# x's row sums on ScalarE, no two-input work on GpSimd, 512-token plain units, and an output projection by columns

## The chip, the core and the metric

The kernel runs on one core of a Trainium2 chip. Its engines are TensorE (PE, matmuls; PEld is its weight load), VectorE (DVE), ScalarE (ACT), GpSimd (POOL) and SyncE (SP), which here only issues DMAs. The metric is device microseconds of one execution; the median of three runs is given. Times in the text are microseconds (us) from the first instruction of the profiled execution.

## The reference

x is 512 tokens x 2048. One decoder layer is computed in float32:

- h = x * rsqrt(mean(x^2) + 1e-6) * gain, then z = h @ w_in with w_in 2048 x 8192.
- z is split into eight blocks of 1024 columns. Four (q, f, i, g) feed 8 heads of HGRN2, a gated linear recurrence with a 128 x 128 state; four (q, k, v, g) feed 16 heads of causal attention with ALiBi, in which three dilated windows are mixed.
- Each branch is multiplied by silu of its gate g; both are laid side by side to y (512 x 2048), then x + y @ w_out, and a last RMSNorm.

## The kernel before

**Arithmetic.** Each float32 operand of a large product is cut into a high and a low part (`cut`, L107 on ACT and L108 on DVE) and a product is three matmuls: hi*hi, hi*lo, lo*hi (L653 to L655, L725 to L727, L955 to L957, L985 to L987).

**Input projection.** The 8192 columns are worked in 32 units of 256 columns (two blocks of 128). x comes transposed in 16 tiles `xt` of 128 features x 512 tokens and is cut by `split_x`. Units 0 to 3 are "plain": 16 steps k, and in each step two blocks x two token halves of 256 (tiles X1, A21, X2, X4), 12 matmuls of 256 columns, in four PSUM banks. The other 28 units use seven products over half-size blocks in place of eight (Strassen's scheme), 24 matmuls of 256 columns each; they need the sums X3, X5, X6, X7, which are built on DVE during units 1 to 3. x's norm is applied after the projection: the row sums of squares are formed beside unit 0 (`square_x`: ACT squares each `xt`, POOL adds into `acc`, a matmul with ones at L248 sums over features), and `rrow` scales each result.

**Mixers.** While the projection of later units runs, the heads of the finished units run in its gaps. Their parts are put at slots by `at_slot(dt, fn)`; `tick()` counts one slot per 12 matmuls of a product (per step k in a plain unit). A HGRN head's `carry` has three two-input multiplies on POOL (L371 to L373), an attention pair's `bias` one scaling and one addition on POOL (L483, L484). `turn` and `turn_values` are PE transposes that wait for a result of DVE or ACT. Each result y goes to DRAM (`y_dram`).

**Output projection.** Columns 0 to 1023 are plain: four passes (kh, n), each over one half of the features and 512 columns, with four PSUM banks that are added into `r` (x, loaded from DRAM) at L960 after each pass. Columns 1024 to 2047 use seven products again. y is read back from DRAM and cut: `y_hgrn` (for kh = 0), `y_attn` (kh = 1), `y_sums` (the sums for the products). `open_out1` loads x's second half, `open_out2` the final gain `fg`, and multiplies the eight finished `r` tiles by it on POOL (L892). `finish` scales the rows and stores.

**Order.** Each engine and each DMA queue runs its instructions in a fixed order. That order is made before the run: a planner takes the program's order and its own estimate of durations, so that an instruction may be issued ahead of earlier ones that are not ready in its estimate; at run time a late input holds up all that is queued behind.

Of the kernel before, what the change touches and what calls it, by code (L numbers as in the profile page):

```python
# [63 lines left out]
def tile_kernel(ctx: ExitStack, tc: tile.TileContext, x, xT, w_in, w_out, gain, lbl, gnorm, fgain,  # L64
# [45 lines left out]
    def x_tiles(m, of=None):  # L110

        return [tuple(xp.tile([P, 4, HS], F32R, tag=f"X{of or m}{p}{t}", name=f"X{m}{p}{t}") for p in "hl")
                for t in range(2)]

# [11 lines left out]
    acc = st.tile([P, S], F32, name="acc")  # L126
    xts = []

    def load_x(upto):
        while len(xts) < min(upto, KT):  # L130
            k = len(xts)
            xt = st.tile([P, S], F32, tag="xt", name=f"xt_{k}", bufs=13)
            nc.sync.dma_start(xt, xT[k * P:(k + 1) * P, :])
            xts.append(xt)

    X = {m: x_tiles(m) for m in (1, 2, 4, 7)}
    A21 = x_tiles(3)
    for m in (6, 5):
        X[m] = x_tiles(m)

    def blocks_of(k):

        return (X[1], A21) if k < KH else (X[2], X[4])

    def split_x(k):
        t, kb = divmod(k % KH, 4)
        g = gain_sb[:, k:k + 1]
        for th, pair in enumerate(blocks_of(k)):
            hi, lo = (a[:, kb] for a in pair[t])
# [4 lines left out]
    def square_x(k):  # L154
        if k == 0:
            A.activation(acc, xts[k], AF.Square)
        else:
            sq = st.tile([P, S], F32, tag="sq", name=f"xsq_{k}", bufs=2)
            A.activation(sq, xts[k], AF.Square)
            G.tensor_add(acc, acc, sq)  # L160

    def x7(k):
        t, kb = divmod(k, 4)
        hi, lo = (a[:, kb] for a in X[7][t])
        g, d = gain_sb[:, k:k + 1], st.tile([P, HS], F32, tag="d7", name=f"d7_{k}", bufs=3)
        V.tensor_sub(d, xts[k][:, :HS], xts[k][:, HS:])
        A.activation(hi, d, AF.Copy, scale=g)
        V.scalar_tensor_tensor(lo, d, g, hi.bitcast(F32), op0=ALU.mult, op1=ALU.subtract)
# [21 lines left out]
    def x3(t):  # L190
        if t == 0:
            X[3] = x_tiles(3)
# [51 lines left out]
    def row_stats():  # L244

        ss = mixer_bank("ss_ps")
        for sb in range(NSB):
            T.matmul(ss[:, sb:sb + 1], acc[:, sb * P:(sb + 1) * P], cs["ones"][:, 0:1], start=True, stop=True)  # L248
        ms = cst.tile([P, NSB], F32, name="ms_x")
        V.tensor_scalar(ms, ss[:, :NSB], 1.0 / D, EPS, op0=ALU.mult, op1=ALU.add)  # L250
# [106 lines left out]
    def work_v(h, src):  # L357
# [5 lines left out]
        def carry():  # L363
# [93 lines left out]
    def work_aq(j, q):  # L457
# [21 lines left out]
        def bias(i):  # L479
# [3 lines left out]
            G.tensor_scalar(nb, H["dist"][:, 0], slope, 0.0, op0=ALU.mult, op1=ALU.add)  # L483
            G.tensor_add(nb, nb, H["dist"][:, 1])  # L484
# [49 lines left out]
    def work_av(j, src):  # L534
# [18 lines left out]
        at_slot(1, turn_values)  # L553
        at_slot(12, values)
# [63 lines left out]
    def plain_unit(u):  # L618
        blocks = UNITS[u]
        banks = [[bank(*tb) for tb in (("a", f"a_{u}"), ("c", f"c_{u}"))],  # L620
                 [bank(*tb) for tb in (("c", f"c2_{u}"), ("t", f"t_{u}"))]]
        for k in range(KT):
            kg, kb = divmod(k, 4)
            t = kg % 2
            if u == 0:
                load_x(k + 8)
                if k == 1:
                    load_plain(0, 1)
                    small_consts()
                for i in range(*((0, 2) if k == 0 else (k + 1, min(k + 2, KT)))):  # L630
                    split_x(i)
                if k >= 1:
                    for i in range(*((0, 1) if k == 1 else (k - 1, k))):
                        square_x(i)
# [12 lines left out]
            for n in range(2):  # L647
                hi, lo = pieces[u, kg, n]
                c = slice(kb * P, kb * P + P)
                for th, pair in enumerate(blocks_of(k)):  # L650
                    xh, xl = (a[:, kb] for a in pair[t])
                    ps = banks[n][th][:, :HS]
                    T.matmul(ps, hi[:, c], xh, start=k == 0, stop=False)  # L653
                    T.matmul(ps, hi[:, c], xl, start=False, stop=False)
                    T.matmul(ps, lo[:, c], xh, start=False, stop=k == KT - 1)  # L655
        if u == 0:
            square_x(KT - 1)
# [3 lines left out]
        for n, (kind, i, _) in enumerate(blocks):  # L661
            z = block_tile(kind, i)
            A.copy(z[:, :HS], banks[n][0][:, :HS])
            V.tensor_copy(z[:, HS:], banks[n][1][:, :HS])
# [93 lines left out]
    Y = {}  # L758
    O = {}

    def staged(k, pool, tag):
        s = pool.tile([P, S], F32, tag=tag, name=f"ys_{k}_{now[0]}", bufs=2)
        nc.sync.dma_start(s, y_dram[k])
        return s
# [5 lines left out]
    def y_tiles(*which):  # L770
        for m, of in which:
            if m not in Y:
                Y[m] = x_tiles(m, of)

    def y_hgrn(kb):
        y_tiles((21, 7), (1, 1))
        h = staged(kb, zp, "zA" if kb % 2 else "zB")
# [3 lines left out]
    def y_attn(kb):  # L781
        y_tiles((2, 2), (4, 4))
        a = staged(KH + kb, O["w2"], "ya")
        cut(*y_parts(2, kb), a[:, :HS])
        cut(*y_parts(4, kb), a[:, HS:])

    def y_sums(kb):

        y_tiles((7, 3), (5, 5), (6, 6), (3, 7))
        h, a = staged(kb, O["w2"], "yh"), staged(KH + kb, O["w2"], "ya")  # L790
        a11, a21, a12, a22 = h[:, :HS], h[:, HS:], a[:, :HS], a[:, HS:]
        V.tensor_sub(a11, a11, a21)
        cut(*y_parts(7, kb), a11)
        V.tensor_sub(a21, a22, a21)
        V.scalar_tensor_tensor(a22, a11, -1.0, a22, op0=ALU.mult, op1=ALU.subtract)
        cut(*y_parts(6, kb), a22)
        V.scalar_tensor_tensor(a12, a12, -1.0, a22, op0=ALU.mult, op1=ALU.subtract)
        cut(*y_parts(3, kb), a12)
        cut(*y_parts(5, kb), a21)

    def after_product(u, m):
        if u == len(UNITS) - 1 and m in (6, 3, 5, 4):
            i = (6, 3, 5, 4).index(m)
            y_hgrn(2 * i)
            y_hgrn(2 * i + 1)
# [7 lines left out]
    OS = [(0, (kh, n), jb) for kh in range(2) for n in range(2) for jb in range(4)]  # L813
# [22 lines left out]
    osteps = [(0, (kh, n), kb) for kh in range(2) for n in range(2) for kb in range(KH)]  # L836
# [21 lines left out]
    def open_out():  # L858
        close(H["acm"])
        close(zp_cm)  # L860
# [4 lines left out]
        for th in range(2):  # L865
            for n in range(2):
                for blk in range(2):
                    r = w2.tile([P, 512], F32, name=f"r0_{th}_{n}_{blk}")
                    sb = 2 * th + blk
                    nc.sync.dma_start(r, x[sb * P:(sb + 1) * P, n * 512:n * 512 + 512])  # L870
                    O["R"][0, th, n, blk] = r

    def open_out1():

        for i, (th, n) in enumerate(((1, 1), (0, 0), (1, 0), (0, 1))):
# [230 lines left out]
```

## Time and profile before

| | |
|---|---|
| median of 3 runs | 1009.81 us (1009.49 to 1012.33) |
| profiled execution | 1009.9 us, span 1008.1 us |
| PE busy | 945.9 us, 94% of the span |
| PEld busy | 888.3 us, 88% |
| DVE busy | 779.3 us, 77% |
| ACT busy | 576.1 us, 57% |
| POOL busy | 199.0 us, 20% |
| mean granted TensorE clock | 0.981 |

A busy share is the part of the span in which an engine had an instruction under way. Matmuls are pipelined, so the distance between the starts of two matmuls, and not the duration of one, says what a matmul costs. In a row, "[2.59 <-DMA r<-x_dram]" is idle time before the instruction and what ended it.

### The profile page before, as it was taken

To read this page: it belongs to the slowest core of one execution; us is meant where nothing else is said; L and a number is where in the kernel's file an instruction comes from. 1 tells how busy PE (TensorE), PEld (TensorE's weight loads), DVE (VectorE), ACT (ScalarE), POOL (GpSimd) and SP (SyncE) were. 2 spreads that over 40 slices of the span, in tenths; PEclk is the share of its full clock that TensorE was granted. 3 is DMA by queue.
4 is the path that set the end of the run, shared out by engine and by line. 5 is a ranking of instruction groups with operands and counts; after the bars stand their busy time and mean duration, and the time that the engine had idled before them with its cause. 6 is when DMAs were issued, how large, how long until landed. Compare 5 with 4: busy or idle time off the path is not lost.

```text
span 1008.1 us, 18861 instructions
## 1 busy us (share of the span) xinstructions
PE 945.9 (94%) x7096; PEld 888.3 (88%) x7096; DVE 779.3 (77%) x1564; ACT 576.1 (57%) x1218; POOL 199.0 (20%) x203
## 2 busy tenths in 40 slices
PE   5899999999999999989999999999999998989795
PEld 5899999999999999988999999999999866768584
DVE  7899869787786878767878787888888835677756
ACT  7554456556464656556667676767666724345345
POOL 5501312121111211112121222221211101001501
PEclk9899999999999999999999999999999999989898
DMA  8133356676766666665666666666666649835634
GB/s 319 53 115 100 80 138 166 158 185 158 180 158 178 158 147 158 157 167 148 161 156 165 156 148 157 152 160 158 161 167 178 200 159 290 275 110 134 180 83 167
DMA packets 51516, 162.34 MB, mean 161 GB/s; under 512 B 5792, under 2 KB 5824, under 8 KB 51424
## 3 DMA queue, kind: packets, MB, share of 16 engines
q1 hardware_dynamic: 36576, 108.02, 31.5%
q0 software_dynamic: 14560, 52.58, 29.0%
q8 instruction: 56, 0.92, 0.4%
q10 hardware_dynamic: 288, 0.52, 0.2%
q14 instruction: 36, 0.29, 0.1%
HBM read 152.72 MB, written 8.39 MB: 160 GB/s over the span
## 4 chain that ended last, share of the span: by engine, by line
PE 62%; DVE 14%; DMA 10%; issue 8%; ACT 3%; POOL 2%; SPq 0%; DVEq 0%; POOLq 0%; ACTq 0%
PE a L725 6%; PE a L727 6%; PE a L726 6%; PE t L725 4%; PE t L727 4%; PE t L726 4%; DMA ys<-yd 3%; PE c L726 3%; PE c L725 3%; PE c L727 3%; DVE lo L108 3%; DMA wB<-w_in_dram 3%; PE ao L547 2%; PE op L955 2%; DVE lo_o L108 2%
## 5 line engine op out<-in xcount | busy, mean ns | idle before, releaser
L107 ACT CAST hi<-wA 128x512 fp32r<-128x512 f32 x168 | 103.3, 619 | 93.9 <-PE a L726 52.6
L108 DVE TENSOR_TENSOR lo<-wA,hi 128x512 fp32r<-128x512 f32 x168 | 114.7, 690 | 18.4 <-ACT hi L107 17.6
L108 DVE TENSOR_TENSOR lo<-wB,hi 128x512 fp32r<-128x512 f32 x112 | 85.5, 771 | 16.6 <-ACT hi L107 16.2
L107 ACT CAST hi<-wB 128x512 fp32r<-128x512 f32 x112 | 68.0, 615 | 49.3 <-PE a L726 19.7
L584 POOL DMA_DIRECT2D wA<-w_in_dram x56 | 49.5, 883 | 141.3 <-DVE lo L108 124.8
L682 DVE TENSOR_TENSOR wA<-wA,wB 128x512 f32<-128x512 f32 x56 | 39.4, 713 | 44.8 <-DMA wB<-w_in_dram 44.8
L725 PE MATMUL t<-X3h,hi 128*128 128x256 f32 x224 | 65.7, 293 | 0.0
L725 PE MATMUL c<-X4h,hi 128*128 128x256 f32 x224 | 65.3, 291 | 0.0
L725 PE MATMUL a<-X1h,hi 128*128 128x256 f32 x224 | 65.1, 291 | 0.0
L725 PE MATMUL a<-X5h,hi 128*128 128x256 f32 x224 | 64.9, 290 | 0.0
L725 PE MATMUL a<-X6h,hi 128*128 128x256 f32 x224 | 64.8, 289 | 0.1
L725 PE MATMUL t<-X2h,hi 128*128 128x256 f32 x224 | 64.1, 286 | 0.0
L725 PE MATMUL c<-X7h,hi 128*128 128x256 f32 x224 | 63.9, 285 | 0.0
L727 PE MATMUL t<-X3h,lo 128*128 128x256 f32 x224 | 63.9, 285 | 0.0
L726 PE MATMUL t<-X3l,hi 128*128 128x256 f32 x224 | 63.9, 285 | 0.0
L726 PE MATMUL a<-X1l,hi 128*128 128x256 f32 x224 | 63.5, 283 | 0.0
L727 PE MATMUL a<-X1h,lo 128*128 128x256 f32 x224 | 63.5, 283 | 0.0
L727 PE MATMUL a<-X6h,lo 128*128 128x256 f32 x224 | 63.4, 283 | 0.0
L727 PE MATMUL t<-X2h,lo 128*128 128x256 f32 x224 | 63.4, 283 | 0.0
L726 PE MATMUL t<-X2l,hi 128*128 128x256 f32 x224 | 63.4, 283 | 0.0
L726 PE MATMUL a<-X5l,hi 128*128 128x256 f32 x224 | 63.3, 283 | 0.0
L727 PE MATMUL c<-X7h,lo 128*128 128x256 f32 x224 | 63.3, 283 | 0.0
(389 smaller groups left out, 3523.0 us busy)
## 6 DMA issues: line engine op xcount, KB each, us to landing
wA<-w_in_dram POOLq DMA_DIRECT2D x56, 512.0 KB, 7.1
wB<-w_in_dram SPq DMA_DIRECT2D x28, 512.0 KB, 4.3
wA<-w_in_dram SPq DMA_DIRECT2D x28, 512.0 KB, 3.5
wD<-w_in_dram SPq DMA_DIRECT2D x28, 512.0 KB, 6.2
wC<-w_in_dram SPq DMA_DIRECT2D x28, 512.0 KB, 5.6
wB<-w_in_dram POOLq DMA_DIRECT2D x28, 512.0 KB, 6.3
os<-w_out_dram SPq DMA_DIRECT2D x24, 512.0 KB, 3.7
ys<-yd SPq DMA_DIRECT2D x32, 256.0 KB, 5.1
```

The source lines that it names most:

```text
L107: A.copy(hi, src)
L108: V.tensor_sub(lo, src, hi.bitcast(F32))
L547: T.matmul(o_ps[64 * i:64 * i + 64, kb * P:], pair["v"][:, kb, 64 * i:64 * i + 64], pt[:, c0:c0 + w], start=kb == 0, stop=kb == 3)
L584: nc.gpsimd.dma_start(raws[u, b], in_tile(u, GROW[b, m]), accum_op=ALU.add)
L682: V.tensor_add(raw_a[:, c], raw_a[:, c], raw_b[:, c])
L725: T.matmul(ps, hi[:, c], xh[:, kb], start=st_, stop=False, skip_group_check=not opens)
L726: T.matmul(ps, hi[:, c], xl[:, kb], start=False, stop=False, skip_group_check=not opens)
L727: T.matmul(ps, lo[:, c], xh[:, kb], start=False, stop=en, skip_group_check=not opens)
L955: T.matmul(ps, xh[:, tok], hi, start=kb == 0, stop=False)
```

## The change

- x's row sums: x is loaded a second time, in rows (eight half-row tiles of 128 x 1024, two buffers), and ACT squares each with a sum along the row (`square_rows`); `square_x`, the POOL additions and the matmul with ones are gone.
- POOL's two-input work goes to DVE: `carry`, `bias` (one instruction in place of two) and the multiplication by `fg`.
- Plain units use 512 tokens per matmul: x's parts are kept in tiles 512 wide (XJ), of which X1, A21, X2, X4 are slices; `split_x` is one ACT and one DVE instruction per k; a unit has two PSUM banks, which alternate.
- Mixer parts that wait for others are moved to later slots.
- The output's plain half is done by columns: two passes n over all 16 k, each with four banks of its own; n = 1 has the mixers' banks. y is read back in pairs, its sums are spread over both passes, and its loads use other buffers. x's second half is loaded later (after step 3 of product 1), and the first evacuation comes after product 1.

```diff
-        for th, pair in enumerate(blocks_of(k)):
-            src = xts[k][:, HS * th:HS * th + HS]
-            A.activation(hi, src, AF.Copy, scale=g)
-            V.scalar_tensor_tensor(lo, src, g, hi.bitcast(F32), op0=ALU.mult, op1=ALU.subtract)
-            A.activation(sq, xts[k], AF.Square)
-            G.tensor_add(acc, acc, sq)
+        hi, lo = (a[:, kb] for a in XJ[k // KH][t])
+        A.activation(hi, xts[k], AF.Copy, scale=g)
+        V.scalar_tensor_tensor(lo, xts[k], g, hi.bitcast(F32), op0=ALU.mult, op1=ALU.subtract)
+    def load_rows():
+        xq = st.tile([P, D // 2], F32, tag="xq", name=f"xq_{sb}_{half}", bufs=2)
+        nc.sync.dma_start(xq, x[sb * P:(sb + 1) * P, half * (D // 2):(half + 1) * (D // 2)])
+    def square_rows(i):
+        A.activation(rows[i], rows[i], AF.Square, accum_out=ssx[:, i // 2, i % 2:i % 2 + 1])
...
-            G.tensor_mul(kv[:, :, 0], p[:, :, 0], e1)
-            G.tensor_mul(qv[:, :, 1], p[:, :, 1], e1)
-            G.tensor_mul(o["ke"], f.rearrange("p (a c) -> p a c", a=NSB), e2)
+            V.tensor_mul(kv[:, :, 0], p[:, :, 0], e1)
+            V.tensor_mul(qv[:, :, 1], p[:, :, 1], e1)
+            V.tensor_mul(o["ke"], f.rearrange("p (a c) -> p a c", a=NSB), e2)
-        for dt, fn in ((1, carry), (2, turn_values), (4, scores), (5, turn), (8, states), (11, outputs), (14, scale),
-                       (16, back)):
+        for dt, fn in ((1, carry), (4, turn_values), (5, scores), (6, turn), (9, states), (12, outputs), (15, scale),
+                       (18, back)):
-            G.tensor_scalar(nb, H["dist"][:, 0], slope, 0.0, op0=ALU.mult, op1=ALU.add)
-            G.tensor_add(nb, nb, H["dist"][:, 1])
+            V.scalar_tensor_tensor(nb, H["dist"][:, 0], slope, H["dist"][:, 1], op0=ALU.mult, op1=ALU.add)
-            at_slot(4 + 2 * n + 3, turn, n // 4, n % 4)
+            at_slot(4 + 2 * n + 4, turn, n // 4, n % 4)
-        at_slot(1, turn_values)
-        at_slot(12, values)
+        at_slot(3, turn_values)
+        at_slot(14, values)
...
-        banks = [[bank(*tb) for tb in (("a", f"a_{u}"), ("c", f"c_{u}"))],
-                 [bank(*tb) for tb in (("c", f"c2_{u}"), ("t", f"t_{u}"))]]
+        banks = [bank("ac"[u % 2], f"p0_{u}"), bank("tc"[u % 2], f"p1_{u}")]
+                if 5 <= k < 13:
+                    load_rows()
+                if k >= 8:
+                    square_rows(k - 8)
...
-        for u, th, n, blk in O["R"]:
-            if u == 0:
-                G.tensor_mul(r, r, O["fg"][0][:, 512 * n:512 * n + 512])
+    def scale_first(n, sb):
+        V.tensor_mul(r, r, O["fg"][0][:, 512 * n:512 * n + 512])
-    def o_plain(kh, n, i0):
-        tags = ("a", "c", "c", "t")
-        ob = [mixer_bank(f"op_{sb}") if kh and n else bank(tags[sb], f"op_{kh}_{n}_{sb}") for sb in range(NSB)]
-        for kb in range(KH):
+    def o_plain(n, i0):
+        tags = ("t", "c", "a", "c")
+        ob = [mixer_bank(f"op_{sb}") if n else bank(tags[sb], f"op_{n}_{sb}") for sb in range(NSB)]
+        for k in range(KT):
...
+    for i in range(4):
+        at_slot((3, 6, 10, 19)[i], y_attn, 2 * i)
+        at_slot((21, 27, 33, 39)[i], y_sums, 2 * i)
+    at_slot(17, open_out0)
+            at_slot(2 * KT * 2 + 18 + 3 * (4 * n + sb), scale_first, n, sb)
```

## Rows read from the trace of the kernel before

**Rows 1.** The page, part 1: busy time, share, instructions of each engine.

```profile
PE 945.9 (94%) x7096; PEld 888.3 (88%) x7096; DVE 779.3 (77%) x1564; ACT 576.1 (57%) x1218; POOL 199.0 (20%) x203
```

**Rows 2.** The waits of PE: who waited for whom, us in total, times, longest.

```profile
PE a L653 <- ACT hi_p L107: 8.9, 1, 8.9
PE vp_h L276 <- DVE v L744: 7.5, 5, 1.7
PE op L955 <- DVE r L960: 6.8, 2, 4.3
PE op L955 <- ACT osq L898: 6.5, 2, 5.8
PE oa L987 <- DVE lo_o L108: 6.3, 1, 6.3
PE p L511 <- ACT pr L502: 4.6, 3, 2.8
```

**Rows 3.** Windows, one per stage: length, each engine's busy us, PEclk, DMA.

```profile
core 0: us, PE busy (x) PEld busy (x) DVE busy (x) ACT busy (x) POOL busy (x), PEclk, DMA share, GB/s
8.80:43.50 34.70, 30.59 (x193) 28.59 (x194) 32.06 (x49) 25.33 (x58) 22.58 (x15) 0.90 0.52 193
43.50:123.40 79.90, 77.36 (x648) 75.79 (x649) 73.58 (x133) 37.85 (x70) 15.08 (x12) 1.00 0.35 96
427.90:798.70 370.80, 363.62 (x2935) 348.70 (x2934) 298.97 (x637) 246.56 (x551) 74.80 (x77) 1.00 0.65 162
798.70:909.00 110.30, 96.69 (x413) 76.25 (x413) 65.03 (x149) 44.94 (x106) 4.69 (x5) 0.94 0.65 203
```

**Rows 4.** Timeline of PE in unit 0: start, us, instruction, count.

```profile
8.88 0.58 PE L653 MATMUL a<-X1h,hi_p 128*128 128x256 f32 x1 [8.88 <-ACT hi_p L107]
...
14.17 0.41 PE L653 MATMUL a<-X1h,hi_p 128*128 128x256 f32 x1
...
36.13 0.28 PE L653 MATMUL a<-X2h,hi_p 128*128 128x256 f32 x1
...
38.53 0.28 PE L655 MATMUL c<-X2h,lo_p 128*128 128x256 f32 x1
```

**Rows 5.** Timeline of PE in the output's plain half.

```profile
840.00 0.39 PE L955 MATMUL op<-hi_o,X21h 128*128 128x512 f32 x1
...
844.53 0.39 PE L957 MATMUL op<-lo_o,X1h 128*128 128x512 f32 x1
...
857.02 0.63 PE L957 MATMUL op<-lo_o,X2h 128*128 128x512 f32 x1
...
860.44 0.63 PE L956 MATMUL op<-hi_o,X4l 128*128 128x512 f32 x1
```

**Rows 6.** Timeline of DVE: in units 0 and 2, and in the seven products.

```profile
28.22 1.51 DVE L152 SCALAR_TENSOR_TENSOR X4l<-xt,gain_sb,X4h 128x256 fp32r<-128x256 f32 x1
...
34.31 0.48 DVE L152 SCALAR_TENSOR_TENSOR X2l<-xt,gain_sb,X2h 128x256 fp32r<-128x256 f32 x1
...
71.21 0.69 DVE L334 TENSOR_TENSOR f<-f,rrow 128x512 f32<-128x512 f32 x1
...
942.73 10.93 DVE L108 TENSOR_TENSOR lo_o<-oA,hi_o 128x512 fp32r<-128x512 f32 x4
```

**Rows 7.** Groups of POOL by line: busy, mean ns, idle time before.

```profile
L160 POOL TENSOR_TENSOR acc<-acc,xsq 128x512 f32<-128x512 f32 x15 | 22.6, 1505 | 16.0 <-ACT xsq L159 15.3
L892 POOL TENSOR_TENSOR r<-r,fg 128x512 f32<-128x512 f32 x8 | 10.7, 1374 | 11.4 <-DMA fg<-fgain_dram 11.4
```

**Rows 8.** Timeline of ACT in unit 0: one square of 512.

```profile
21.68 0.62 ACT L159 ACTIVATE xsq<-xt 128x512 f32<-128x512 f32 x1
```

**Rows 9.** DMA issues by line: size, median us from issue to landing.

```profile
ys<-yd SPq DMA_DIRECT2D x32, 256.0 KB, 5.1
wp<-w_in_dram SPq DMA_DIRECT2D x14, 512.0 KB, 3.9
dist<-consts_dram POOLq DMA_DIRECT2D x1, 512.0 KB, 9.6
```

More of the change, by code (lines that the diff above doesn't have):

```diff
@@ L244, in row_stats @@
     def row_stats():
-        ss = mixer_bank("ss_ps")
-        for sb in range(NSB):
-            T.matmul(ss[:, sb:sb + 1], acc[:, sb * P:(sb + 1) * P], cs["ones"][:, 0:1], start=True, stop=True)
         ms = cst.tile([P, NSB], F32, name="ms_x")
-        V.tensor_scalar(ms, ss[:, :NSB], 1.0 / D, EPS, op0=ALU.mult, op1=ALU.add)
+        V.tensor_add(ms, ssx[:, :, 0], ssx[:, :, 1])
+        V.tensor_scalar(ms, ms, 1.0 / D, EPS, op0=ALU.mult, op1=ALU.add)
         rstd = rsqrt_small(cst, ms, NSB, "x")
@@ L646, in plain_unit @@
                     cut_w(2)
-            for n in range(2):
+            for n, ps in enumerate(banks):
                 hi, lo = pieces[u, kg, n]
                 c = slice(kb * P, kb * P + P)
[L650 to L655, printed above, removed]
+                xh, xl = (a[:, kb] for a in XJ[k // KH][t])
+                T.matmul(ps, hi[:, c], xh, start=k == 0, stop=False)
+                T.matmul(ps, hi[:, c], xl, start=False, stop=False)
+                T.matmul(ps, lo[:, c], xh, start=False, stop=k == KT - 1)
         if u == 0:
-            square_x(KT - 1)
             row_stats()
@@ L768, in y_parts, with y_cut @@
         return tuple(a[:, b] for a in Y[m][t])
[L770 to L773, printed above, removed]
+    def y_cut(m, kb, src):
+        t, b = divmod(kb, 4)
+        cut(*(a[:, b:b + 2] for a in Y[m][t]), src)
     def y_hgrn(kb):
-        y_tiles((21, 7), (1, 1))
-        h = staged(kb, zp, "zA" if kb % 2 else "zB")
+        h = staged([kb], zp, "zA" if kb % 2 else "zB", 2)[:, 0]
         cut(*y_parts(21, kb), h[:, HS:])
@@ L781, in y_attn, with first, second, y3 @@
     def y_attn(kb):
[L782 to L785, printed above, removed]
+        a = staged([KH + kb, KH + kb + 1], wp, "wC", W_BUFS["C"])
+        y_cut(2, kb, a[:, :, :HS])
+        y_cut(4, kb, a[:, :, HS:])
     def y_sums(kb):
[L789 to L799, printed above, removed]
+        h, a = staged([kb, kb + 1], O["w2"], "yh", 1), staged([KH + kb, KH + kb + 1], O["w2"], "ya", 1)
+        a11, a21, a22 = h[:, :, :HS], h[:, :, HS:], a[:, :, HS:]
+        def first():
+            V.tensor_sub(a22, a22, a21)
+            y_cut(5, kb, a22)
+            V.tensor_sub(a21, a11, a21)
+        def second():
+            y_cut(7, kb, a21)
+            V.scalar_tensor_tensor(a11, a22, -1.0, a11, op0=ALU.mult, op1=ALU.subtract)
+            y_cut(6, kb, a11)
+        at_slot(4, first)
+        at_slot(6, second)
+    def y3(t):
+        (h6, l6), (h12, l12) = whole(Y[6], t), whole(Y[2], t)
+        d = O["w2"].tile([P, 4, HS], F32, tag=("yh", "ya")[t], name=f"y3_{t}")
+        V.scalar_tensor_tensor(d, h6, -1.0, h12, op0=ALU.mult, op1=ALU.subtract)
+        V.tensor_sub(d, d, l6)
+        V.tensor_sub(d, d, l12)
+        cut(*Y[3][t], d)
     def after_product(u, m):
[L802 to L805, printed above, removed]
+        if u == len(UNITS) - 1 and m in (3, 5, 4):
+            for kb in {3: (0, 1), 5: (2, 3), 4: (4, 5)}[m]:
+                y_hgrn(kb)
     oraw = {}
@@ L960, in o_plain @@
             V.tensor_add(r, ps, r)
-            if kh:
-                squares(0, sb // 2, n, sb % 2)
+            squares(0, sb // 2, n, sb % 2)
     def o_product(m, i0):
@@ L977, in o_product @@
             for kb in range(KH):
-                o_cut(i0 + kb + 5)
+                tick()
+                if not last:
+                    o_cut(i0 + kb + 5)
                 hi, lo = ocuts[i0 + kb]
```

160 lines of the change are left out of this document (85 added, 75 removed).

## The prediction

> **What bounds the kernel now.** I read the busy shares first. PE has 94% and its weight load 88% [rows 1], so PE sets the time nearly everywhere, and what can be won is what PE loses: idle time, half-clock time, and matmuls in a form that costs more than it must. The second view is the waits of PE [rows 2]: six lines hold 40.6 us of idle time, among them 8.9 before the first matmul (inputs), 7.5 in five transposes of v, 19.6 in the output projection (6.8 + 6.5 + 6.3) and 4.6 in attention's transposes. Third, the windows by stage [rows 3]: in unit 0 PE is busy 30.6 of 34.7 us at a mean clock of 0.90 while DVE is busy 32.1; in units 1 to 3 DVE has 73.6 of 79.9; in the attention part PE has 363.6 of 370.8 and DVE 299.0; in the output's first part PE has only 96.7 of 110.3 at a clock of 0.94.
>
> Last, timelines say what a matmul costs. Two starts of 256-wide matmuls 20 apart, 36.13 and 38.53, give 0.120 each [rows 4]; two of 512-wide ones 20 apart, 840.00 and 844.53, give 0.2265, so 0.113 per 256 columns [rows 5]. At the lower granted clock (1.2 GHz) eight starts from 857.02 to 860.44 give 0.43 [rows 5]; this follows the 4.3 us gap, the longest of [rows 2]'s third line. And DVE's two-input instruction of 256 takes 0.48 us at 34.31, but 1.51 at 28.22, when POOL adds into acc [rows 6, 7]; four cuts of 512 take 10.93 us at 942.73, while POOL multiplies by fg, against 0.69 for one such instruction at 71.21 [rows 6]. POOL's two-input work thus holds DVE up threefold, and DVE holds up PE.
>
> **The change, part by part**, against the profiled execution: 1009.9 us, its span 1008.1 and 1.8 around it; the median of the runs, 1009.81, is the same to 0.1.
>
> *Unit 0.* Removed: 32 splits of 256 on DVE, at 0.48 or 1.51, and POOL's 15 additions of 1.5 us. Added: 16 splits of 512 at 0.69. DVE's work drops to 11 us of splits, some 5.5 for the 8 weight cuts and 3 of small things, 20 in all. PE needs 96 x 0.2265 = 21.7 us. The half-clock start stays: 24 intervals from 8.88 to 14.17 [rows 4] are 0.22 each in place of 0.12, a loss of 2.4. PE could end at 8.9 + 21.7 + 2.4 = 33.0 instead of 43.5, 10.5 us sooner. Against it: the weight cuts are now ahead of the splits in ACT's program order (up to 1 us later), and the squares. A 1024-wide square is not in the trace; one of 512 takes 0.62 [rows 8], so it costs between that and twice that, and I take 0.9: eight make 7 us, less than the 16 x 0.62 that go. They need 4 MB more through SP's queue in two buffers. A 512 KB load lands in 3.9 us [rows 9], so four rounds of load and square are about 4 x (3.9 to 6 + 0.9) = 19 to 28 us, from about 12: the last sum is ready at 31 to 40, around unit 0's end. Behind it wait DVE's row statistics and the PE matmuls of rrow; a late one costs PE up to 7 us. I take a gain of 7.5, ends 2 and 10.5.
>
> *Units 1 to 3.* Each has 192 x 0.120 = 23.0 against 96 x 0.2265 = 21.7, 1.3 less, 3.9 for three. Short waits at unit ends have less cause with alternating banks; they count nothing here. But DVE is 92% busy there [rows 3] and gets the carry of the first heads (two 256-wide and one 512-wide multiply, 0.48 + 0.48 + 0.69 = 1.65 per head [rows 6]). So I take 4, ends 0 and 5. The Trainium skill ("TensorE: Matmul & The Clock Gate", Back-to-back issue gap) gives 262 cycles for a 256-wide and 518 for a 512-wide matmul at 2.4 GHz; by that estimate a unit would win only 192 x 0.109 - 96 x 0.216 = 0.2 us, and the total would be some 4.5 us higher. The trace has 0.120 for the narrow form, with the weight load busy nearly all of the time (75.8 of 79.9) [rows 3], so the row decides here.
>
> ACT and DVE now empty the two halves of one bank. The Trainium skill ("PSUM — Partial Sum Buffer", PSUM bank collisions raise a hardware error) says two engines must not be in one bank at once, so the two copies follow each other. No run so far shows this here. By rows it is one more copy, below 0.69 us, for each of eight banks: 5.5 us if PE waited for all of them, nothing while the other unit's two banks take the next matmuls, and I take nothing.
>
> *Heads.* turn_values moves from slot 2 to 4 after v is ready, almost 3 us later; the wait is at most 1.7 [rows 2], so the 7.5 go. DVE's added 8 x 1.65 = 13 us of carry replaces POOL work that had slowed it; it lies beside matmuls. I take 7.5, ends 6 and 7.5.
>
> *Attention.* turn one slot (12 x 0.120 = 1.4 us) later removes most of the 4.6 us [rows 2]. bias moves to DVE: 16 x 0.69 = 11 us on an engine with 72 us idle in that stretch [rows 3]. Its first use waits for dist, whose load takes 9.6 us [rows 9]; that wait stood on POOL, where nothing followed, and now stands on DVE, where the weight cuts follow. Four pieces of lookahead are 4 x 1.4 = 5.7 us, so this can cost PE up to 4. I take a gain of 3, ends 4.6 and minus 4.
>
> *Output projection.* A pass now has its own banks, so the 13.3 us of waits for r and osq go [rows 2]; with them go two half-clock stretches of about 11 matmuls, 11 x (0.43 - 0.2265) = 2.2 each [rows 5]: 17.7. y's loads land in 5.1 us [rows 9]; attention's y is needed from k = 8, 16 slots in, instead of 32, but its loads are at slots 3 to 19 and the last pair has 9 slots, 12 us, between load and use: hidden. In the products 6.3 us and a half-clock 2.2 go with POOL's multiply, but in its place DVE multiplies, queued for the fg load that POOL waited 11.4 us for [rows 7], with the first one only two slots (12 x 0.2265 = 2.7 us) behind its issue; x's second half is loaded four steps of six matmuls (5.4 us) later than before too, and its subtraction also stands on DVE ahead of the cuts. Five pieces of lookahead cover 6.8 us, so some 5 of a 9 us wait come through to PE. I take 17.7 + 8.5 - 8.2 = 18, ends 8 and 26.
>
> The start (8.9) and the tail after the last matmul are left alone. Sum: 7.5 + 4 + 7.5 + 3 + 18 = 40, so 1009.9 - 40 = 970.
>
> **Rivals.** (a) *The waits move to DVE rather than going.* POOL's waits for dist, fg and the row sums become DVE's, and x's rows come late. For it: the 9.6 and 11.4 us loads [rows 9, 7] and DVE's 92% in units 1 to 3 [rows 3]. Against: lookahead of four to five pieces. Price: the low ends of unit 0, units 1 to 3, attention and output: 2 + 0 + 6 - 4 + 8 = 12, so 998; midway to the forecast, 984. (b) *Everything works.* All high ends: 10.5 + 5 + 7.5 + 4.6 + 26 = 54, so 956, and short waits that I left out a few us more. For it: each wait is named in [rows 2] and each has its edit. (c) *Slower: DVE becomes the engine PE waits for in the 28 product units.* Carry and bias put 13 + 11 us on it. If a pair of units were held by its DVE chain once, PE idles and comes back at 1.2 GHz: 1.5 us of wait and 2.2 of clock, 3.7 for each of 14 pairs is 52 us, above the other gains of 40, so 1022. It decides where pieces arrive later than four slots ahead. Against: DVE is at 81% there [rows 3], the addition is 3%, POOL's interference goes, and no wait of a product for a cut stands among the lines read [rows 2]. (d) *It does not do what it says:* the contention is not what held unit 0 and the output, DMA landings were; then 7.5 + 4 and half the output's 18 remain: 989.
>
> **Chances and range.** Forecast (961 to 978) 0.50; (a) 0.18; (b) 0.15; (c) 0.07, which I count with every way to be slower at 0.08; (d) 0.09. A change below 0.3% (3 us) can't be told from none. Faster 0.88, within 0.04, slower 0.08. The range takes in (b) and most of (a) and (d): 950 to 992; left out are the worst of (a), and (c).
>
> **What would show it.** In the profile after: POOL without L160, L371 to L373, L484, L892; splits of 512 near 0.69 throughout and unit 0's last matmul by 36; plain units 22 us apart; no wait of vp_h for v; no wait of op for r or osq and a clock of 1.00 in the first output stretch. Wrong would be: PE waiting for rrow, for nb through DVE at the first attention pair, or for lo_o while DVE sits before its multiply by fg; or the splits still at 1.5 us with POOL idle.

## The result and the profile after

The changed kernel takes 988.2 us (median of 4 runs, 986.9 to 989.8); the kernel before, run beside it, 1011.1 (1009.5 to 1013.2). The ratio is 0.9773, 95% interval 0.9747 to 0.98: 23 us faster, where 40 were forecast. The profiled execution spans 986.1 us, 22.0 less than before. The page of the changed kernel, busy time, answers to [rows 1]: TensorE's own work fell by 11 us, GpSimd's by half.

```profile
PE 934.6 (95%) x6704; PEld 861.8 (87%) x6704; DVE 753.0 (76%) x1549; ACT 558.9 (57%) x1176; POOL 103.3 (10%) x124
```

The first matmul of each stage, read from PE's timeline of both kernels, splits the 22.0 us:

| stage | before | after | gain | forecast |
|---|---|---|---|---|
| unit 0 | 34.5 | 24.6 | +9.9 | 7.5 |
| units 1 to 3 | 80.0 | 76.8 | +3.2 | 4 |
| heads | 304.5 | 299.4 | +5.1 | 7.5 |
| attention | 370.8 | 382.3 | -11.6 | +3 |
| output to its last matmul | 198.5 | 183.1 | +15.4 | 18 |
| start, tail | 19.8 | 19.9 | 0 | 0 |

Four terms have the right sign and lie within 3 us of the forecast (the heads below the low end stated, 6); attention went the other way and accounts for nearly all that is missing. The waits of PE after (who for whom: us in all, times, longest) answer to [rows 2]:

```profile
PE p L660 <- ACT hi_p L107: 8.9, 1, 8.9
PE a L733 <- DVE lo L108: 8.7, 1, 8.7
PE ot L1009 <- DVE lo_o L108: 4.3, 2, 2.9
PE s L496 <- DVE Q L477: 4.1, 1, 4.1
PE rrow_ps L268 <- DVE dg L267: 2.6, 1, 2.6
PE p L516 <- ACT pr L507: 1.7, 4, 0.8
```

The waits for v, r and osq are gone. Three have come or grown: a weight cut in the first attention unit (8.7), Q in the last (4.1), rrow in unit 1 (2.6, 0.9 before). The wait of the output's products for lo_o moved from the fourth product (6.3) to the third (4.3). The windows by stage (length, busy time of each engine, granted clock, DMA share, GB/s) answer to [rows 3]: unit 0, units 1 to 3, attention, the output's plain half:

```profile
8.80:33.50 24.70, 24.55 (x96) 20.01 (x97) 21.16 (x47) 21.40 (x41) 0.00 (x0) 1.00 0.85 310
33.50:110.30 76.80, 73.09 (x351) 58.69 (x351) 65.78 (x123) 38.43 (x70) 5.27 (x6) 1.00 0.46 138
409.80:792.10 382.30, 365.80 (x2934) 351.22 (x2933) 298.20 (x658) 242.07 (x550) 38.72 (x46) 0.98 0.65 160
792.10:891.20 99.10, 95.10 (x426) 75.04 (x426) 61.19 (x104) 41.21 (x83) 3.41 (x4) 1.00 0.68 216
```

In unit 0 PE is busy throughout, the clock reads 1.00 (but see the last section) and POOL does nothing. In attention PE's busy time hardly changed (363.6 before), but 16.5 us are idle and the mean clock is 0.98. What stands before the two attention waits is seen in two timelines. DVE, first attention unit: the bias (L489) waits for dist, the table of distances that it is made from, and the weight cut behind it (wA, like wB and wC below, is a tile of weights) comes 10 us after the one before.

```profile
418.80 0.69 DVE L108 TENSOR_TENSOR lo<-wA,hi 128x512 fp32r<-128x512 f32 x1
426.37 0.69 DVE L489 SCALAR_TENSOR_TENSOR nb<-dist 128x512 f32<-128x512 f32 x1 [6.87 <-DMA dist<-consts_dram]
...
429.21 0.69 DVE L108 TENSOR_TENSOR lo<-wA,hi 128x512 fp32r<-128x512 f32 x1
```

ACT, last attention unit: a cast of y for the output waits 4.8 us for its load, with both casts of Q behind it.

```profile
767.60 0.41 ACT L107 CAST Xuh<-ys 128x256 fp32r<-128x256 f32 x1
772.81 0.41 ACT L107 CAST X7h<-ys 128x256 fp32r<-128x256 f32 x1 [4.80 <-DMA ys<-yd]
...
773.43 1.25 ACT L476 CAST Q<-aq 64x512 fp32r<-64x512 f32 x2
```

### The profile page after: what moved, and what is told of

The parts are those of the page before. It is cut to its first block, busy times and chain, and to the rows that moved or that the text cites. A ratio compares the mean times of both kernels' runs of the same rounds, so it can differ in the third digit from the quotient of the medians.

```text
span 986.1 us, 17902 instructions
## 1 busy us (share of the span) xinstructions
PE 934.6 (95%) x6704; PEld 861.8 (87%) x6704; DVE 753.0 (76%) x1549; ACT 558.9 (57%) x1176; POOL 103.3 (10%) x124
## 4 chain that ended last, share of the span: by engine, by line
PE 42%; DMA 26%; DVE 15%; issue 10%; ACT 3%; POOL 2%; SPq 0%; POOLq 0%; DVEq 0%; ACTq 0%
DMA wB<-w_in_dram 15%; DVE lo L108 5%; DMA ys<-yd 4%; PE a L731 4%; DMA wA<-w_in_dram 4%; PE a L733 4%; PE a L732 4%; PE t L733 3%; PE t L731 3%; PE t L732 3%; PE c L731 2%; PE c L733 2%; PE c L732 2%; DMA os<-w_out_dram 2%; ACT hi L107 1%
## 5 line engine op out<-in xcount | busy, mean ns | idle before, releaser
L733 PE MATMUL t<-Xvh,lo 128*128 128x256 f32 x224 | 63.9, 285 | 2.2 <-DVE lo L108 2.2
L731 PE MATMUL t<-Xuh,hi 128*128 128x256 f32 x224 | 64.8, 289 | 0.5
L731 PE MATMUL a<-Xuh,hi 128*128 128x256 f32 x224 | 65.0, 290 | 0.0
L732 PE MATMUL a<-X6l,hi 128*128 128x256 f32 x224 | 64.5, 288 | 0.0
L731 PE MATMUL c<-Xvh,hi 128*128 128x256 f32 x224 | 64.3, 287 | 0.0
L731 PE MATMUL t<-Xvh,hi 128*128 128x256 f32 x224 | 64.1, 286 | 0.0
L732 PE MATMUL t<-Xul,hi 128*128 128x256 f32 x224 | 63.7, 284 | 0.0
L733 PE MATMUL t<-Xuh,lo 128*128 128x256 f32 x224 | 63.7, 284 | 0.0
L733 PE MATMUL c<-Xvh,lo 128*128 128x256 f32 x224 | 63.4, 283 | 0.0
L733 PE MATMUL a<-X5h,lo 128*128 128x256 f32 x224 | 63.3, 283 | 0.0
```

The lines of the kernel that those rows point to most:

```text
L731: T.matmul(ps, hi[:, c], xh[:, kb], start=st_, stop=False, skip_group_check=not opens)
L732: T.matmul(ps, hi[:, c], xl[:, kb], start=False, stop=False, skip_group_check=not opens)
L733: T.matmul(ps, lo[:, c], xh[:, kb], start=False, stop=en, skip_group_check=not opens)
```

## The experiments

All are variants of the changed kernel. Stages in us from one profile each; "ratio" is to the kernel before, run beside it, with its 95% interval. Stages that an edit doesn't touch differ by 2 to 5 us between profiles (heads 296.9 to 301.7, first attention unit 31.8 to 34.6, third product 16.0 to 19.5), so a difference of that size is read only where a wait or a row goes with it. The profiled execution is not always near the median: with three edits it took 963.5, the fastest of six.

| kernel | median | ratio | unit 0 | unit 1 | 2, 3 | heads | att. first | att. later | att. last | out passes | third product |
|---|---|---|---|---|---|---|---|---|---|---|---|
| before | 1011.1 | 1 | 34.5 | 26.1 | 53.9 | 304.5 | 28.9 | 317.4 | 24.5 | 112.5 | 10.9 |
| after | 988.2 | 0.975-0.980 | 24.6 | 26.5 | 50.3 | 299.4 | 34.0 | 318.2 | 30.2 | 99.2 | 17.8 |
| bias on GpSimd | 989.8 | 0.978-0.985 | 24.4 | 26.3 | 50.0 | 300.1 | 26.8 | 325.2 | 31.3 | 99.7 | 17.1 |
| dist early | 982.4 | 0.970-0.974 | 24.6 | 27.3 | 50.0 | 300.3 | 23.1 | 322.3 | 30.4 | 99.2 | 17.5 |
| Q before y | 982.4 | 0.969-0.975 | 23.3 | 27.7 | 50.0 | 299.6 | 34.6 | 320.2 | 27.8 | 96.6 | 17.7 |
| late evacuation | 986.8 | 0.975-0.981 | 24.0 | 26.5 | 50.3 | 301.7 | 32.0 | 317.9 | 29.9 | 98.7 | 17.8 |
| spread loads | 982.5 | 0.970-0.976 | 24.4 | 26.6 | 50.3 | 300.7 | 33.2 | 318.0 | 31.6 | 100.6 | 12.1 |
| sums on GpSimd | 994.6 | 0.982-0.989 | 34.9 | 23.8 | 50.2 | 296.9 | 31.8 | 319.7 | 29.3 | 98.8 | 19.5 |
| narrow plain | 994.5 | 0.981-0.987 | 24.7 | 31.4 | 52.1 | 297.7 | 32.9 | 319.6 | 29.5 | 98.3 | 18.5 |
| slots back | 976.4 | 0.962-0.969 | 23.7 | 28.8 | 50.0 | 300.2 | 30.5 | 314.9 | 25.5 | 99.1 | 16.0 |
| slots back, carry on GpSimd | 984.1 | 0.971-0.977 | 23.5 | 29.3 | 53.2 | 305.5 | 30.9 | 313.3 | 27.4 | 97.3 | 17.2 |
| turn back alone | 979.2 | 0.967-0.973 | 25.3 | 26.2 | 50.3 | 300.0 | 33.1 | 314.4 | 29.8 | 97.3 | 17.2 |
| three edits | 969.3 | 0.957-0.963 | 23.4 | 27.6 | 50.1 | 299.8 | 25.8 | 313.9 | 26.5 | 98.1 | 10.9 |
| three, rrow later | 965.9 | 0.953-0.959 | 24.1 | 23.4 | 51.5 | 301.5 | 26.7 | 314.8 | 25.6 | 97.2 | 10.9 |

**The wait for dist: bias on GpSimd again, and dist loaded early.**

```diff
-            V.scalar_tensor_tensor(nb, H["dist"][:, 0], slope, H["dist"][:, 1], op0=ALU.mult, op1=ALU.add)
+            G.tensor_scalar(nb, H["dist"][:, 0], slope, 0.0, op0=ALU.mult, op1=ALU.add)
+            G.tensor_add(nb, nb, H["dist"][:, 1])
```

> The changed kernel with the bias computed on GpSimd again (its two instructions), everything else as changed; dist is still loaded when attention opens, so it lands as late as in the changed kernel. In the changed kernel the 8.7 us gap of TensorE in the first attention unit (34.0 us from its first matmul to the next unit's, 28.9 before the change) lies behind a VectorE wait of 6.9 us for dist. Theory: the wait itself costs nothing, only the weight cuts queued behind it on VectorE do; on GpSimd the wait stays some 7 to 11 us long, the gap goes, the unit falls to 28 to 30 us and the run to 982 to 985. Rival: the unit's own weights come late (ScalarE waited 4.4 us for wB there): a gap of 4 us or more stays at the same place and the run stays at 986 to 989.

```diff
+        H["ecm"], ds = open_pool("ds")     # before the first head
+        H["dist"] = ds.tile([P, 2, S], F32, name="dist")
+        nc.gpsimd.dma_start(H["dist"], consts[:, 256:].rearrange("p (a c) -> p a c", a=2))
```

> The changed kernel with dist in a buffer of its own that is loaded when the first head opens, some 350 us ahead of its use; the bias stays on VectorE. Theory: no instruction of the first attention unit waits for dist, VectorE's 6.9 us of idle time and TensorE's gap of 8.7 us go with its half-clock stretch, the unit falls from 34.0 to 25 to 28 us and the run to 979 to 982. Rival (weights late there): a gap of about 4 us stays and the run is at 984 to 986. Second rival: GpSimd's queue, without the 512 KB load among the weights' loads, changes nothing: the unit stays at 34.

With the bias on GpSimd dist is as late as ever: POOL waits 9.0 us for it. PE's gap of 8.7 shrinks to one of 2.3, and the unit takes 26.8 us: the place in VectorE's queue cost the time, as the theory has it. The run did not follow (989.8, single runs from 986.5 to 998.3, expected 982 to 985): the later pairs took 7.0 us more. Where one of DVE's weight cuts meets the bias addition there, it takes 1.79 us in place of 0.69; PE waits seven times for DVE ahead of scores, 4.0 us in all. Timelines of POOL and of DVE, second pair, bias on GpSimd:

```profile
423.17 0.62 POOL L489 TENSOR_SCALAR nb<-dist 128x512 f32<-128x512 f32 x1 [9.04 <-DMA dist<-consts_dram]
...
486.80 0.69 DVE L108 TENSOR_TENSOR lo<-wB,hi 128x512 fp32r<-128x512 f32 x1
...
488.05 1.55 POOL L490 TENSOR_TENSOR nb<-nb,dist 128x512 f32<-128x512 f32 x1
...
488.37 1.79 DVE L108 TENSOR_TENSOR lo<-wB,hi 128x512 fp32r<-128x512 f32 x1
```

(The first line is that of POOL's wait for dist, in the first pair.) So with the later slots the move of the bias was worth about 7 us in the later pairs, which the prediction had at nothing, and lost about 7 in the first. With the sooner slots it is worth less: the kernel before (317.4) and the one with the slots back (314.9) differ by 2.5 there. With dist early the first unit takes 23.1 us, no gap above 0.2 is left in it, and the run falls to 982.4. The 10.9 us are the gap of 8.7 and what followed it: from 430.0 to 434.5 the granted clock was 0.50, the lower of its two levels, which costs 2.3. The later pairs took 4.1 us more than in the changed kernel; that isn't explained.

**The wait for Q.** Only the order of issue on ScalarE is fixed.

```diff
+                with tc.issue_after(H["q cast"].ins):   # kb 2 to 5
                     y_hgrn(kb)
```

> The changed kernel with one order of issue fixed: on ScalarE, the casts of y's recurrent blocks 2 to 5 stand behind the last attention pair's casts of Q. In the changed kernel one such cast waits 4.8 us for its load (4.4 us from issue to landing, behind a buffer) with Q's casts queued behind it, and TensorE then waits 4.1 us for Q; that stretch, from the last unit's first matmul to the output's first, takes 30.2 us, 24.5 before the change. Theory: the order alone costs it; the wait for Q goes, the stretch falls to 25 to 27 and the run to 983 to 985. Rival: y's loads themselves are late (they start only when a buffer comes free), and the same time is lost at the output's first matmuls: the stretch falls, but the output's first pass takes 3 to 5 us more, and the run stays at 987 to 989.

The wait for Q fell from 4.1 to 0.4 us, the stretch by 2.3 (27.8, expected 25 to 27; 29.3 or more in every other run with the later slots). The output passes didn't pay for it (96.6), so the rival falls. Part of the stretch stays lost: other casts of y wait for their loads (1.3 and 2.6 us) ahead of a copy that PE needs. Waits of PE in that stretch, first line:

```profile
PE a L731 <- ACT ag L745: 2.4, 1, 2.4
```

**The output's third product.** First the two sums that DVE waits in are put behind weight cuts.

```diff
-                for blk in blks:
-                    evacuate(1, 7, blk, O["c"][blk])
+                at_slot(4, late, 7, "c")      # late: evacuate both blocks, issued behind the last weight cut
+                at_slot(5, late, 1, "a")
```

> The changed kernel with the two sums of the output's first two products into the second half of x put later: on VectorE they stand behind the weight cuts of the fourth and fifth step of the third product. In the changed kernel VectorE waits 5.0 and 3.3 us for that half of x there, and the third product takes 17.8 us against 10.9 of its neighbours. Theory: x's late load is what holds the cuts; the third product falls to 11 to 12.5 and the run to 982 to 984. Rival: the load of the final gain is just as late, and the multiplies by it, which now come first, hold the cuts instead: the third product stays above 15 us and the run at 986 to 989.

Third product 17.8, unchanged: the theory falls. The rival saw half of it: DVE now waits for fg, but what PE waits for (one gap of 5.2) is ScalarE's cut, which waits 10.9 us for its weights. Timelines of DVE and of ACT, late evacuation:

```profile
918.98 1.29 DVE L913 TENSOR_TENSOR r<-r,fg 128x512 f32<-128x512 f32 x2 [4.59 <-DMA fg<-fgain_dram]
...
924.58 1.14 ACT L107 CAST hi_o<-os 128x512 fp32r<-128x512 f32 x2 [10.92 <-DMA os<-w_out_dram]
```

The changed kernel has the same wait of ACT, hidden behind DVE's; its eight loads of x (256 KB) there land in 11.8 us, where y's tiles of that size took 5.1 [rows 9]. ACT's timeline, then the DMA issues from 900 to 932 us:

```profile
925.69 1.14 ACT L107 CAST hi_o<-os 128x512 fp32r<-128x512 f32 x2 [10.72 <-DMA os<-w_out_dram]
```

```profile
r<-x_dram SPq DMA_DIRECT2D x8, 256.0 KB, 11.8
```

In that view the DMA engines are some 90% busy from 902 to 925 us, and everything asked for is late together. So the transfers were spread (the multiplies by fg and the first product's sum, not shown here, go behind weight cuts too):

```diff
+                    if th == n == 0:
+                        nc.sync.dma_start(*args)
+                    else:
+                        at_slot({(1, 0): 8, (1, 1): 12, (0, 1): 16}[th, n] + 2 * blk, late, "os", nc.sync.dma_start, *args)
-            if m == 1:
+            if m == 2:
                 open_out2()
```

> The changed kernel with the transfers around the output's third product spread out: of the second half of x only the two tiles that the third product needs are loaded in the second one, the other six later, each behind a load of weights in SyncE's queue; the final gain is loaded one product later, and its eight multiplies and the first product's sum go behind weight cuts of the fourth and fifth product. In the run with the late evacuation the third product stayed at 17.8 us and TensorE waited for ScalarE's cut instead, which waited 10.9 us for its weights, while the DMA engines were over 90% busy. Theory: 2 MB of x, 1 MB of gain, 2 MB of accumulated weights and the next weights are all asked for within 14 us, and the transfers together are late; spread out, the third product takes 11 to 12.5 us, none of the later products grows by more than 1 us, and the run is at 981 to 983. Rival: the weights are late by their own issue, which waits for a buffer; then the third product stays above 15 us and the run at 986 to 989.

Third product 12.1, the three after it 0.5 us longer together, run 982.5: the theory's numbers are met, its reason is not. The first two tiles of weights (os) land no sooner after their issue (10.8 and 10.6 us; 10.1 and 8.9 in the changed kernel). They are issued 5 us sooner, counted from the output's first product (891.24 in the changed kernel, 894.11 here): in SyncE's queue they stand behind two loads of x in place of eight. So the rival has half of it, the weights' own issue, though what it waited behind was x's loads and not a buffer. Timelines of SP, changed kernel and spread loads:

```profile
907.53 5.73 SPq L901 DMA_DIRECT2D r<-x_dram  x8
915.50 12.80 SPq L839 DMA_DIRECT2D os<-w_out_dram  x4
```

```profile
910.63 1.01 SPq L907 DMA_DIRECT2D r<-x_dram  x2
913.14 13.24 SPq L839 DMA_DIRECT2D os<-w_out_dram  x4
```

The sums and multiplies were moved in the same edit; what each part is worth was not separated.

**Unit 0: the sums of squares back on GpSimd.**

```diff
+            G.tensor_add(acc, acc, sq)       # 15 times; load_rows and square_rows are not called
```

> The changed kernel with one part undone: x's sums of squares come from the transposed x again, squared on ScalarE and added up by GpSimd, and x is not loaded in rows. Wide splits, wide matmuls and early weight cuts stay. Theory of the prediction (GpSimd's two-input additions hold VectorE up): VectorE's 512-wide splits rise from 0.7 us to well over 1 us on the mean while GpSimd adds, and unit 0 rises from 24.6 us to 30 to 34; unit 1 loses its wait for rrow (2 to 4 us less), so the run is at 991 to 996. Rival (DMA landings held unit 0): the splits stay below 0.9 us, unit 0 stays at 24 to 26 us, and the run is at 984 to 987.

Unit 0 takes 34.9 us, as before the change, and the splits are long again (group of DVE from 8 to 45 us, busy, mean ns; 748 in the changed kernel; the seven of Xul took 1041 and 747):

```profile
L151 DVE SCALAR_TENSOR_TENSOR Xvl<-xt,gain_sb,Xvh 128x512 fp32r<-128x512 f32 x8 | 11.6, 1510 | 0.0
```

So unit 0's gain comes from the new way to the row sums, and by the length of the splits from taking GpSimd's additions away; the rival (landings) falls. The price is in unit 1: without x's rows to load it takes 23.8 us, 2.8 less, and the wait for rrow is 0.5 in place of 2.6.

**Narrow matmuls in the plain units.**

```diff
+                for w in (slice(0, HS), slice(HS, S)):
+                    T.matmul(ps[:, w], hi[:, c], xh[:, w], ...)    # and the two others
```

> The changed kernel with each 512-wide matmul of the four plain units cut into two of 256 into the two halves of the same bank; splits, cuts and banks stay. By the rows of the kernel before, 192 narrow matmuls take 192 x 0.120 = 23.0 us and 96 wide ones 96 x 0.2265 = 21.7: each unit rises by 1.3 us, the third plain unit from 22.0 to 23.3, the run by some 4 to 5 us, 992 to 994. Rival (a narrow matmul issues in about half a wide one's time): 0.2 us for a unit, and the run stays at 987 to 990.

Units 2 and 3, which take 50.0 to 50.3 us in all runs that leave them alone, rise by 1.1 and 0.8, close to the 1.3 of the rows; unit 1 by 4.9, since it also waits 4.7 us for rrow; the run is at 994.5. Three narrow starts in unit 2 are 0.12 apart:

```profile
70.01 0.29 PE L663 MATMUL p<-Xuh,lo_p 128*128 128x256 f32 x1
70.13 0.28 PE L661 MATMUL p<-Xuh,hi_p 128*128 128x256 f32 x1
70.25 0.28 PE L662 MATMUL p<-Xul,hi_p 128*128 128x256 f32 x1
```

By an estimate from the cycles that the Trainium skill ("TensorE: Matmul & The Clock Gate", Back-to-back issue gap) gives for isolated matmuls, 262 and 518, the two forms are within 0.2 us for a unit; the rows differ by 1 us, and the measurement decides.

**The slots: all back, then with the carry on GpSimd, then the turn alone.**

```diff
-        for dt, fn in ((1, carry), (4, turn_values), (5, scores), (6, turn), (9, states), (12, outputs), (15, scale), (18, back)):
+        for dt, fn in ((1, carry), (2, turn_values), (4, scores), (5, turn), (8, states), (11, outputs), (14, scale), (16, back)):
-            at_slot(4 + 2 * n + 4, turn, n // 4, n % 4)
+            at_slot(4 + 2 * n + 3, turn, n // 4, n % 4)
-        at_slot(3, turn_values)
-        at_slot(14, values)
+        at_slot(1, turn_values)
+        at_slot(12, values)
```

> The changed kernel with the slots of the mixer's steps put back: v is turned two slots after it is ready (one in attention), the probabilities three slots after their scores, the heads' later steps one slot sooner. Theory of the prediction: TensorE waits for v (7.5 us over the heads) and for the probabilities (4.6 us in attention) again, and the run rises to 993 to 1000. Rival for attention, from the run with the bias on GpSimd (there the pairs after the first took 7 us more than in the changed kernel, and before the change they took no more with the bias on GpSimd and the sooner slots): the later slots cost in attention what the bias on VectorE gives; then the pairs after the first fall from 318 us to 311 to 314, the heads still rise by 5 to 7, and the run stays at 987 to 992.

Both theories fall, and the run is the best of the single edits: 976.4, 11.8 below the changed kernel. The heads don't change (300.2). Attention falls in all three parts (3.5, 3.2 and 4.7 us). In the first part the gap behind dist is 5.1 in place of 8.7, in the last the wait for Q is gone: the later slots had a share in both. Neither wait that they were to remove came back. Lines of PE's waits, slots back:

```profile
PE p L516 <- ACT pr L507: 1.4, 3, 0.9
...
PE vp_h L282 <- DVE v L750: 0.5, 2, 0.3
```

For the probabilities this is not the last word: PE's gap for dist stands just ahead of their first turns here, and with dist early ("Together", below) the wait does come back. For the heads something else had removed it, the carry:

```diff
-            V.tensor_mul(kv[:, :, 0], p[:, :, 0], e1)      # and the two others
+            G.tensor_mul(kv[:, :, 0], p[:, :, 0], e1)
```

> The kernel with the mixer's slots back, and with the three multiplies of the carry on GpSimd again, as before the change. With the slots back alone, the heads took 300.2 us and TensorE's waits for v 0.5 us in all; before the change 304.5 and 7.5. Theory: what took the waits for v away is that GpSimd's two-input multiplies no longer run beside VectorE's work, not the later slots; then several waits for v come back, 4 to 8 us in all, and the heads take 303 to 306 us, the run 979 to 983. Rival (the carry on VectorE has no part in it): the heads stay at 299 to 301 and the run at 975 to 978.

The waits for v are back at 7.2 us in five places, the heads at 305.5: before, they were 7.5, 5 and 304.5. But it is not mainly slow instructions, as the theory had it. VectorE, with the carry gone, comes early to the sum of two weight tiles, waits for wB's load, and v's subtraction stands behind that sum, another one and two cuts. (Whether the later slots would remove the waits with the carry on GpSimd was not tested.) Units 2 and 3 take 53.2 us, 3.2 more than with the slots back alone. Line of PE's waits, then DVE's timeline in one of the five places:

```profile
PE vp_h L282 <- DVE v L750: 7.2, 5, 1.7
```

```profile
205.76 1.02 DVE L688 TENSOR_TENSOR wA<-wA,wB 128x512 f32<-128x512 f32 x1 [1.69 <-DMA wB<-w_in_dram]
...
208.51 0.74 DVE L750 SCALAR_TENSOR_TENSOR v<-a,v 128x256 f32<-128x256 f32 x2
```

```diff
-            at_slot(4 + 2 * n + 4, turn, n // 4, n % 4)
+            at_slot(4 + 2 * n + 3, turn, n // 4, n % 4)
```

> The changed kernel with one of the slots back: the probabilities are turned three slots after their scores, not four; values, v and the heads keep the later slots. With all slots back the attention stretches fell from 34.0, 318.2 and 30.2 us (first unit, the following, the last) to 30.5, 314.9 and 25.5, the first output pass from 52.0 to 49.6, and the run to 976.4. Theory A: the later turn alone costs it; then the four fall to about those numbers and the run to 976 to 979. Theory B: the later values (and with them the last pair's multiplies and stores of y, ahead of the output) cost it; then the last unit stays at 29 to 31 with its wait for Q, and the run at 984 to 988.

979.2, between the two. A holds for the later pairs (314.4) and the first output pass (50.2), not for the first unit (33.1). B holds for the time of the last unit, 29.8, but its wait for Q is 1.3 and a wait of 3.5 for the probabilities has come. The 3.8 us in the later pairs are in no long wait (none above 0.7 in the changed kernel) but in the places of the matmuls (last section).

**Together.** The slots' edit, dist early and the spread loads; then the matmuls of rrow three steps later in unit 1:

```diff
         if u == 0:
             row_stats()
-            row_stats_along()
+            at_slot(12, row_stats_along)    # what needs rrow, and open_heads, x5, x6, behind it
```

> Three edits together: the mixer's slots back, dist loaded early into a buffer of its own, the transfers around the output's third product spread out. Alone they gave 976.4, 982.4 and 982.5 us, against 988.2 for the changed kernel. Theory: they act in different stretches. From the slots' run, the first attention unit falls from 30.5 to about 23.5 and the third product of the output from 16.0 to 12.1: 976.4 - 7 - 4 = 965, between 963 and 968. Rival: part of it is lost in the later attention pairs, which took 4 us more with dist early alone: 968 to 972.

> The three edits, and the four matmuls that spread x's row scales along the columns put behind the twelfth step of unit 1 in TensorE's order (in the changed kernel they stand behind the ninth and wait 2.6 us for the sums of x's rows, and unit 1 takes 26.5 us against 22.0 for unit 2); what follows from them on VectorE moves along. Theory: the sums are ready in time, TensorE doesn't wait, unit 1 falls by 3 to 4.5 us and the run is that much below the one without this edit: 961 to 964. Rival: what moves along on VectorE is late for units 2 and 3, which grow by as much: within 1 us of the run without it.

969.3, above the theory's range: the third product is at 10.9 and the later pairs do not grow, but the first attention unit is at 25.8 (expected 23.5). There the probabilities are turned sooner than with dist early alone, and PE waits for them again. PE's timeline, three edits:

```profile
432.52 0.55 PE L513 MATMUL p<-cc,pr 128*128 128x128 f32 x3 [2.57 <-ACT pr L504]
```

With rrow later unit 1 falls by 4.2 and the wait is gone, units 2 and 3 grow by 1.4. The run is at 965.9, ratio 0.9558 (0.9531 to 0.9585), below both kernels; that it is below the one without this edit (by 3.3 on the medians) is not clear of the noise, since the runs overlap (963.2 to 967.1 and 963.5 to 972.0). Its waits of PE, the first lines:

```profile
PE p L657 <- ACT hi_p L107: 8.4, 1, 8.4
PE p L513 <- ACT pr L504: 3.6, 3, 2.3
PE y L442 <- ACT os L437: 3.0, 3, 1.5
PE op L988 <- DVE lo_o L108: 2.9, 3, 2.2
```

## Why the prediction was right, and where it was not

*The bound and the sign* were right: PE sets the time, its idle time was what could be won, and DVE did not become the bound of the products (rival c; DVE's waits there are for ACT and wB). That rival's price, a lower clock after a wait of 1.5 us, was not in the rows either: behind the five waits for v, 1.2 to 1.7 us, the granted clock stayed at 1.00 before the change.

*Unit 0* (7.5; measured 9.9). The mechanism is shown by the sums on GpSimd: 34.9 against 24.6. It ended 0.6 below the high end, with the last matmul before 33.5, and the late sums of x's rows, charged to unit 0, were waited for in unit 1: the last was ready at 45.9, not at 31 to 40 (a square and the reading of its sum take 1.25 us, not 0.9, and the first loads of x's rows took 7.2).

*Units 1 to 3* (4; 3.2). Units 2 and 3 gained 3.6 together, 1.9 of it from wide matmuls by the narrow run; the carry, counted as a burden there, helped too (3.2 more with it on GpSimd). Unit 1 got the wait for rrow, which the list of wrong signs named. ACT's and DVE's copies of one bank never overlap in the plain units (34.44 for 0.36 us, then 35.17), and PE starts the next unit meanwhile. That agrees with the Trainium skill ("PSUM — Partial Sum Buffer", PSUM bank collisions raise a hardware error), and nothing was the right price.

*Heads* (7.5; 5.1). Near in size, but not for the reason given. "turn_values moves from slot 2 to 4 after v is ready ... so the 7.5 go": they go with the old slots too, and come back with the carry on GpSimd. The carry, which the step counted as a cost beside matmuls, was the gain; that the later slots would have done it without the carry is not shown.

*Attention* (3; -11.6) is the step that failed, in three terms, which overlap. (1) "this can cost PE up to 4": the wait for dist cost about 7 to 11 (bias back on GpSimd 7.2, dist early 10.9). Lookahead was set against the wait alone, but after it four instructions of the pair, the bias among them, went ahead of the first cut (426.37 to 429.21), and dist landed 11.3 us after its issue, not 9.6. (2) "turn one slot (...) later removes most of the 4.6 us": in the first unit it does (4.0 before the change, none with dist early, 2.6 with dist early and the sooner slots), but the later slots had a price, and that was put at nothing: 11 us over attention, of which 3.5 lie in the first unit, with its gap behind dist, and 4.7 in the last, with its wait for Q. The bias off GpSimd, worth 7 in the later pairs with these slots and less with the sooner ones, was priced at nothing too. (3) The wait for Q, 4.1 us, was in no term. Casts of y for the output were issued ahead of attention's last work, and with the slots back they are not in the way; why the later slots put them there was not tested. The prediction looked at y's loads for the output's need alone ("hidden").

*Output* (18; 15.4). The passes gained 13.3 of 17.7: the waits for r and osq are gone and the clock reads 1.00, but short waits for cuts and for ag remain (3.0 in all). In the products the 8.5 came (32.7 us for the three after the third, 41.4 before), and against it "some 5 of a 9 us wait come through": the third product lost 6.9 of the 8.2 in the sum (how 5 became 8.2 the prediction doesn't say). The size is near, the cause another: x's eight loads stand ahead of the third product's weights in SyncE's queue, as the spread loads show, and fg is only one of the transfers that are late with them.

The forecast itself, 970 (961 to 978), is missed by 18 us; the stated range, 950 to 992, holds the result because it takes in most of rival (a). The measured time lies where rival (a) had it (984 to 998), and two of its waits came, dist on DVE and the row sums; but the slots and the wait for Q, as large as these, were in no case, so that the time fits rival (a) is in part luck. Rival (d)'s 989 is near by chance: its mechanism falls with the sums on GpSimd.

## What to carry to other kernels

A wait that moves to another engine is priced by what stands behind it in that engine's queue until PE's next need, not by its length less the lookahead. An edit that ships in a bundle should be credited with a wait's end only if the other edits couldn't have ended it: here the heads' later slots took credit for what moving the carry off GpSimd did. A wait can also hide behind a longer one, as that for the probabilities did behind dist, so an edit taken back should be tried again once the longer wait is gone. And moving a step later is a change of order on every engine: look at what now runs ahead of what.

## What the runs showed of the hardware

- The first 13 wide matmuls of the changed kernel start 0.43 us apart, the later ones 0.2265. The windows read a granted clock of 1.00 from 8.8 us on, but the trace's first clock record, of the full level, begins at 14.71 us, and the distance falls just there, behind the matmul at 14.66; before it there is no record. In the other profiles the two also fall together (14.45 and 14.38 before the change, 11.71 and 11.72 with three edits). The 0.43 is what the kernel before shows at a recorded 0.50 (857.02 to 860.44), so a start at the lower level, as the prediction had it, fits, and the 1.00 ahead of the first record shows nothing.
- A DVE cut that starts while GpSimd adds ends 0.56 us after GpSimd's instruction does (490.16 against 489.60), as if it had waited for it; the cut before took 0.69. The Trainium skill ("SBUF — State Buffer", SBUF: two separate sides) says that GpSimd and a VectorE instruction with two SBUF inputs take turns at a shared port for a whole instruction each; these rows agree.
- The successor of a matmul that stands right behind transposes starts 82 to 85 ns later, whatever the width: over the later pairs a product's takes 202 ns there against 120 (turn back alone), a score's 143, 202, 260 and 317 for 128 to 512 columns (changed kernel) against 58, 119, 175 and 232 behind a product (turn back alone). With the later turn 39 of the 51 recorded first score matmuls stand there, and 32 fewer product matmuls. Adding up the distances between all starts of the later pairs, score matmuls take 21.3 us with the later turn and 15.6 with the turn back alone, product matmuls 1.7 and transposes 0.2 less: these are the 3.8 us.
